# Encoder layer on one core: half of the input projection as twelve unit pairs by seven block products, values with 512 moving columns, chains moved beside keys, queries and gates

## The chip, the cores and the metric

The kernel runs on one core of a Trainium2 chip. The metric is the device time of one execution in microseconds; the median of several runs counts. The engines are called as in the profile: PE or TensorE for matmuls (PEld for its weight loads), DVE or VectorE, ACT or ScalarE, POOL or GpSimd, SP or SyncE. The last two, and ScalarE at times, issue DMAs.

## The reference

One encoder layer is applied to two request groups that share the weights: a prompt of 256 tokens and a sample of 1024 tokens, with 1024 channels, in float32.

```python
h = rmsnorm(x, g_mix_pre)
z = h @ w_in                                  # 1024 x 9216
rq, rk, rv, rg, pin, mq, gl = jnp.split(z, list(IN_SPLITS), axis=-1)
gates = jax.nn.sigmoid(gl)                    # three gates of 1024 channels
y_ret = retention_branch(rq, rk, rv, rg, decay_fwd, decay_bwd, ret_gn) @ w_ret_out
y_pool = pool_branch(pin, pool_w, pool_scale) @ w_pool_out
y_mem = memory_branch(mq, mem, g_mem, w_mem_kv) @ w_mem_out
merged = gates[:, :, 0] * y_ret + gates[:, :, 1] * y_pool + gates[:, :, 2] * y_mem
x = x + rmsnorm(merged @ w_o, g_mix_post)
x = x + rmsnorm(conv_ffn(rmsnorm(x, g_ffn_pre), w_up, conv_w, conv_b, w_down), g_ffn_post)
```

Retention has 4 heads of 256 channels, rotary positions on q and k, and a decay in both directions; its output is normalised per head and multiplied by silu(rg). Pooling takes means over windows of 2, 4, 8 and 16 tokens minus the token, in four groups of 256 channels, each followed by a 256 x 256 product. The memory branch is softmax attention of mq over 256 memory tokens, whose keys and values come from `w_mem_kv`.

## The kernel before

**Numbers and matmuls.** Every float32 operand x is split into hi = x rounded to the short float format (`hilo`: a ScalarE copy) and lo = x - hi (a VectorE subtraction). `mm3` makes one product of three matmuls, hi x hi, hi x lo and lo x hi, on lines 148 to 150. All 1280 tokens are handled together (`T`), as the groups 512, 512 and 256 of `GROUPS`.

**Weights.** `Weights` streams the weight units (128 x 1024) in a fixed order, the list `srcs`: loaded by SP into two raw tiles, split into a ring of four (lines 87 and 88). A unit is taken when it is needed (`take`), and `tick` refills the ring, so that in steady work one unit is split at the first tick of each unit.

**Feature-major units.** One unit gives 128 output columns for all tokens: three groups of 24 matmuls with the weight as the stationary side (`fm_groups`), 48 with 512 and 24 with 256 moving columns. Values are token-major: per head and per pair of token tiles, 48 matmuls with 256 moving columns (memory values likewise, line 470).

**Chains in the background.** While TensorE works through units, generators in `bg` take one step at each `tick`, and so put their matmuls between the groups. All is issued in this order; nothing is reordered later. `drain` ticks until `bg` is empty. The stages, in order:

1. Memory keys (8 units) and memory values; beside them the statistics of x and the split inputs `hT`, and the decay tables (`decay_tables`), `dtab` among them.
2. `mq` units (8) and values (4 x 2 units); beside them `mem_chain`: 20 jobs of scores, softmax, transposes and the product with the values.
3. `pool_unit` x 8, `rotary_unit` x 4 for q, x 4 for k; beside them `pool_chain`. Its step for one half of a group makes log2(w) shifted sums, edge products, a difference and a split; the products with `pool_w` follow when both halves are there.
4. `rg` units (8); beside them `state_chain`, 16 jobs.
5. 24 gate units; beside the first 22 `ret_chain`, 20 chunks (4 heads x 5). After three preparing steps each chunk takes two, `scores` and (`transp` of the chunk before) `output` with `split` of the next chunk behind it. The tick after the third group is left out for the chain (line 960), but in the first unit.
6. The three branches' output projections, `w_o`, then the MLP. Its up-projection multiplies the sample's 2 x 2 blocks (two halves of tokens, two of channels, a gate unit and a value unit) with seven products instead of eight, on weight sums that stand in DRAM.

**Weight sums.** `sums` makes `s12_d` and `s34_d` for the 22 pairs of up-projection units in five stages per pair, one stage per tick: two DRAM to DRAM copies by SP, then four accumulating DMAs by POOL, each two rounds behind the one that it needs.

**Banks.** `ps_mm` has four PSUM banks for units, `ps_ch` four for chains.

Of the kernel before, what the change touches and what calls it, by code (L numbers as in the profile page):

```python
# [8 lines left out]
F32 = mybir.dt.float32  # L9
# [8 lines left out]
P = 128  # L18
# [20 lines left out]
PCOLS = PW - 2 * PAD  # L39
SLOT = 2 * T  # L40
# [18 lines left out]
class Weights:  # L59
# [8 lines left out]
    def load(self):  # L68
        if self.n_load < self.load_limit and self.n_load < self.n_split + self.RAW:
            t = self.pool.tile([P, 1024], F32, tag="wr", name="wr", bufs=self.RAW)  # L70
            self.nc.sync.dma_start(out=t, in_=self.srcs[self.n_load])
            self.raw[self.n_load] = t
            self.n_load += 1
# [22 lines left out]
    def take(self, n=1):  # L96
# [7 lines left out]
        return out  # L104

# [5 lines left out]
def encoder(ctx: ExitStack, tc: tile.TileContext, a: dict):  # L111
# [68 lines left out]
    w_in = a["w_in"]  # L180
    srcs = [a["w_kv"][i] for i in range(16)]
    srcs += [w_in[40 + i] for i in range(8)]
    srcs += [w_in[16 + i] for i in range(8)]
    for h in range(H):
        srcs += [w_in[32 + 2 * h], w_in[33 + 2 * h], w_in[2 * h], w_in[2 * h + 1]]
    srcs += [w_in[8 + i] for i in range(8)]
    srcs += [w_in[24 + i] for i in range(8)]
    srcs += [w_in[48 + i] for i in range(24)]
# [4 lines left out]
    s12_d = [dram.tile([P, 2, 512], F32, name=f"s12d{q}") for q in range(NF)]  # L193
    s34_d = [dram.tile([P, 2, 512], F32, name=f"s34d{q}") for q in range(NF)]
# [4 lines left out]
    for nm, q in stream:  # L199
        srcs.append({"u0": a["w_up"][q], "a2": a["w_up"][NF + q],  # L200
                     "s12": s12_d[q][:].rearrange("p a b -> p (a b)"),
                     "s34": s34_d[q][:].rearrange("p a b -> p (a b)")}[nm])
# [24 lines left out]
    vm_d = [dram.tile([P, 4, HD], F32, name=f"vm{h}") for h in range(H)]  # L227
    q_d = [dram.tile([P, NCH, 2, C], F32, name=f"qd{h}") for h in range(H)]
    k_d = [dram.tile([P, NCH, 2, C], F32, name=f"kd{h}") for h in range(H)]
    v_d = [dram.tile([P, NCH, 2, HD], F32, name=f"vd{h}") for h in range(H)]  # L230
# [12 lines left out]
    def sums():  # L243
        lag = 2

        def stage(i, q):
            u, v = (a["w_up"][n].rearrange("p (a b) -> p a b", b=512) for n in (q, NF + q))
            both = lambda x: x.unsqueeze(1).to_broadcast([P, 2, 512])
            s12, s34 = s12_d[q], s34_d[q]
            if i == 0:  # L250
                nc.sync.dma_start(out=s12[:], in_=both(v[:, 0, :]))
                nc.sync.dma_start(out=s34[:], in_=u)
            elif i == 1:
                nc.gpsimd.dma_start(out=s12[:], in_=both(v[:, 1, :]), accum_op=ALU.add)
            elif i == 2:
                nc.gpsimd.dma_start(out=s34[:, 0, :], in_=v[:, 0, :], accum_op=ALU.add)
            elif i == 3:
                nc.gpsimd.dma_start(out=s12[:, 1, :], in_=u[:, 0, :], accum_op=ALU.add)
            else:
                nc.gpsimd.dma_start(out=s34[:, 1, :], in_=s12[:, 1, :], accum_op=ALU.add)  # L260

        for n in range(NF + 4 * lag):
            for i in range(5):
                q = n - lag * i
                if 0 <= q < NF:
                    stage(i, q)
                    yield

    summing = [None]

    def tick(step=True):
        ws.tick()
        if summing[0] is not None:
            next(summing[0], None)
# [13 lines left out]
    ds = ExitStack()  # L288
    dec = ds.enter_context(tc.tile_pool(name="dec", bufs=1))
# [62 lines left out]
    def x_stats():  # L352
# [15 lines left out]
        xrb = s0.tile([P, T], F32, name="xrb")  # L368
# [27 lines left out]
    dtab = dec.tile([P, H, 2, C], F32, name="dtab")  # L396

    def decay_tables():
# [24 lines left out]
        nc.vector.tensor_scalar(out=kd, in0=kd, scalar1=HD ** -0.5, scalar2=None, op0=ALU.mult)  # L423
        yield
        rel = s0.tile([P, 2, 2 * C], F32, name="rel")
        nc.sync.dma_start(out=rel, in_=a["rel"])
        for h in range(H):
# [6 lines left out]
            yield  # L434

# [4 lines left out]
    with tc.tile_pool(name="st0", bufs=3) as stp:  # L440
# [21 lines left out]
        for h in range(H):  # L462
            w2 = ws.take(2)
            for j in range(2):
                b = mmb(2, HD)
                for i in range(2):
                    ts = slice((2 * j + i) * P, (2 * j + i + 1) * P)
                    for c in range(KC):
                        wh, wl = (w[:, (c % 4) * HD:(c % 4 + 1) * HD] for w in w2[c // 4])
                        mm3(b[:, i, :], memT[c][:, 0, ts], memT[c][:, 1, ts], wh, wl, c == 0, c == KC - 1)  # L470
                o = stp.tile([P, TM], F32, tag="st", name="st")
                for i in range(2):
                    nc.scalar.activation(o[:, i * HD:(i + 1) * HD], b[:, i, :], AF.Copy,
                                         scale=mrs[:, 2 * j + i:2 * j + i + 1])
                nc.gpsimd.dma_start(out=vm_d[h][:, 2 * j:2 * j + 2, :],
                                    in_=o[:].rearrange("p (a b) -> p a b", b=HD))
                tick()
# [18 lines left out]

# [1262 lines left out]
```

## Time and profile before

| what | value |
|---|---|
| median of 3 runs | 2686.07 us (2685.98 to 2686.65) |
| the profiled execution's own time | 2684.68 us |
| its span, first to last instruction | 2682.9 us |
| mean granted TensorE clock | 0.996 |
| busy: PE, PEld | 2644.3 us (99%), 2293.8 us (85%) |
| busy: DVE, ACT, POOL | 1351.0 us (50%), 919.0 us (34%), 279.2 us (10%) |
| DMA | 397.58 MB, mean 148 GB/s |

Busy time of PE counts overlapping matmuls once. A matmul's own length (0.39 us for 512 columns) is longer than the distance to the next one, since matmuls overlap; the cost of one is that distance. The granted clock is given as a share of 2.4 GHz.

### The profile page before, as it was taken

Reading aid. Unit: us, or ns where it says so; the run is one execution under the profiler, and the core shown is the slowest. Engines: PE = TensorE matmul, PEld = TensorE weight load, DVE = VectorE, ACT = ScalarE, POOL = GpSimd, SP = SyncE. Lnnn points to the kernel's source line nnn. Section 1 sums busy time; section 2 is a strip of 40 time slices with the busy share of each in tenths; the row PEclk is TensorE's granted clock in tenths of the full one; section 3 lists DMA queues with packets and bytes.
Section 4 is the critical chain, followed back from the end, with each engine's and each line's share of the span. In section 5 each row is a group of like instructions: output and inputs, shape, how many; then the busy total and the mean of one; then the engine's idle time right before and its main releaser. Section 6 shows DMA issues by size and latency. Waiting matters only on the chain.

```text
span 2682.9 us, 36263 instructions
## 1 busy us (share of the span) xinstructions
PE 2644.3 (99%) x14396; PEld 2293.8 (85%) x14396; DVE 1351.0 (50%) x2267; ACT 919.0 (34%) x1567; POOL 279.2 (10%) x457
## 2 busy tenths in 40 slices
PE   8999999999999999999999999999999999999998
PEld 6999998888888888888888888777888888878786
DVE  5645303445445355555423453567666566554454
ACT  5433311221124333232312021665344444434333
POOL 1111221211123111111100000110000000000000
PEclk9999999999999999999999999999999999999999
DMA  7775566665478544444434353453333333353443
GB/s 262 260 193 143 138 158 159 153 166 138 126 177 218 167 147 163 138 155 154 155 105 149 111 156 102 145 177 99 113 111 111 113 116 106 128 184 127 149 147 110
DMA packets 145435, 397.58 MB, mean 148 GB/s; under 512 B 17680, under 2 KB 27792, under 8 KB 144912
## 3 DMA queue, kind: packets, MB, share of 16 engines
q1 hardware_dynamic: 100128, 267.02, 30.9%
q0 software_dynamic: 44848, 127.95, 17.6%
q8 instruction: 113, 1.85, 0.3%
q14 instruction: 58, 0.48, 0.1%
q10 hardware_dynamic: 288, 0.28, 0.0%
HBM read 303.69 MB, written 143.39 MB: 167 GB/s over the span
## 4 chain that ended last, share of the span: by engine, by line
PE 93%; DMA 2%; DVE 2%; ACT 2%; issue 1%; SPq 0%; POOL 0%; DVEq 0%; ACTq 0%; POOLq 0%
PE f L1316 15%; PE mm L149 13%; PE mm L148 13%; PE mm L150 13%; PE f L150 10%; PE f L149 10%; PE f L148 10%; PE ch L149 3%; PE ch L150 3%; PE ch L148 3%; DMA wr<-w_kv_in 1%; DMA x<-x2d 0%; DVE wl L88 0%; PE ch L559 0%; PE f L1142 0%
## 5 line engine op out<-in xcount | busy, mean ns | idle before, releaser
L148 PE MATMUL mm<-b,wh 128*128 128x512 f32 (+1 forms) x1536 | 545.7, 355 | 0.0
L149 PE MATMUL mm<-b,wh 128*128 128x512 f32 (+1 forms) x1536 | 544.3, 354 | 0.0
L150 PE MATMUL mm<-b,wl 128*128 128x512 f32 (+1 forms) x1536 | 543.6, 354 | 0.0
L88 DVE TENSOR_TENSOR wl<-wr,wh 128x1024 fp32r<-128x1024 f32 x244 | 297.7, 1223 | 411.6 <-ACT wh L87 407.3
L87 ACT ACTIVATE wh<-wr 128x1024 fp32r<-128x1024 f32 x244 | 255.2, 1050 | 281.5 <-PE f L149 150.7
L150 PEld LDWEIGHTS mm<-b,wl 128*128 128x128 f32 x1536 | 290.1, 189 | 40.9
L148 PEld LDWEIGHTS mm<-b,wh 128*128 128x128 f32 x1536 | 290.4, 189 | 39.1
L149 PEld LDWEIGHTS mm<-b,wh 128*128 128x128 f32 x1536 | 290.4, 189 | 38.3
L1316 PE MATMUL f<-b,wh 128*128 128x512 f32 x880 | 273.9, 393 | 0.0
L1316 PEld LDWEIGHTS f<-b,wh 128*128 128x128 f32 x880 | 161.9, 189 | 30.7
L1316 PE MATMUL f<-b,wl 128*128 128x512 f32 x440 | 171.7, 390 | 0.0
L150 PE MATMUL f<-wh,gl 128*128 128x512 f32 x390 | 153.3, 393 | 5.7 <-DVE gl L141 5.5
L148 PE MATMUL f<-wh,gl 128*128 128x512 f32 x390 | 152.8, 392 | 1.5 <-ACT gl L140 1.5
L149 PE MATMUL f<-b,wh 128*128 128x512 f32 (+1 forms) x432 | 153.4, 355 | 0.0
L148 PE MATMUL f<-b,wh 128*128 128x512 f32 (+1 forms) x432 | 153.1, 354 | 0.0
L150 PE MATMUL f<-b,wl 128*128 128x512 f32 (+1 forms) x432 | 152.8, 354 | 0.0
L149 PE MATMUL f<-wl,gl 128*128 128x512 f32 x390 | 152.7, 392 | 0.0
L141 DVE TENSOR_TENSOR gl<-b,gl 128x640 fp32r<-128x640 f32 x78 | 63.9, 825 | 116.2 <-ACT gl L140 116.1
L964 ACT ACTIVATE gate<-mm 128x512 f32<-128x512 f32 (+1 forms) x68 | 35.5, 522 | 223.6 <-PE mm L150 132.9
L140 ACT ACTIVATE gl<-b 128x640 fp32r<-128x640 f32 x78 | 57.3, 739 | 158.6 <-PE f L150 152.0
L1316 PE MATMUL f<-hc,wh 128*128 128x512 f32 x352 | 108.9, 391 | 0.0
L148 PE MATMUL f<-h2p,wh 128*128 128x256 f32 x352 | 99.9, 284 | 3.3 <-ACT h2p L140 3.3
(343 smaller groups left out, 5295.4 us busy)
## 6 DMA issues: line engine op xcount, KB each, us to landing
wr<-w_in_in SPq DMA_DIRECT2D x72, 512.0 KB, 3.9
wr<-w_up_in SPq DMA_DIRECT2D x44, 512.0 KB, 3.6
wr<-w_down_in SPq DMA_DIRECT2D x44, 512.0 KB, 3.6
b<-fgd SPq DMA_DIRECT2D x44, 320.0 KB, 4.8
h2s<-gtd SPq DMA_DIRECT2D x48, 256.0 KB, 3.8
s12d<-w_up_in SPq DMA_DIRECT2D x22, 512.0 KB, 6.4
s34d<-w_up_in SPq DMA_DIRECT2D x22, 512.0 KB, 7.4
s12d<-w_up_in POOLq DMA_DIRECT2D x22, 512.0 KB, 7.5
```

The lines of the kernel that those rows point to most:

```text
L87: self.nc.scalar.activation(h, r[:], AF.Copy)
L88: self.nc.vector.tensor_tensor(out=l, in0=r[:], in1=h.bitcast(F32), op=ALU.subtract)
L140: nc.scalar.activation(hi, src, AF.Copy)
L141: nc.vector.tensor_tensor(out=lo, in0=src, in1=hi.bitcast(F32), op=ALU.subtract)
L148: nc.tensor.matmul(out, ah, bh, start=first, stop=False)
L149: nc.tensor.matmul(out, ah, bl, start=False, stop=False)
L150: nc.tensor.matmul(out, al, bh, start=False, stop=last)
L964: nc.scalar.activation(y[:, 0:n], b, AF.Sigmoid)
L1316: nc.tensor.matmul(b, w[x][:, ks], hterm(nm, c, y), start=first and c == k == 0, stop=last and c == 3 and k == 2, skip_group_check=True)
```

## The change

Three things are changed. (1) The units of `mq`, `pin` and `rg` (24 of 72) become twelve pairs ("quads"), worked before all chains: on the sample tokens by seven block products of 12 matmuls with 512 columns, on the prompt plainly. Their weights are the first unit, the last unit and two sums made in DRAM by the same `sums` as before, which now has 34 pairs; a load of a sum runs the generator until that sum is complete. Results go through DRAM (`mq_d`, `pin_d`, `g_d`), the block terms of the tokens are made from `xT` while the values are computed (`in_terms`). (2) Values and memory values are computed with 512 moving columns, four, one, one and four token tiles at a time (`token_major`). (3) The chains move: memory beside keys (k) and one gate, pooling and the decay matrix beside nine gates, states beside q, retention beside the gates that are left. Keys and queries tick after each group of each unit; beside the retention chain a gate unit also steps in the middle of its first group (`mid`) and after every group.

```diff
+    def hold(self, i):
+        while self.n_split <= i:
+            assert self.can_split()
+            self.split()
+        return self.hl[i]
+
+    def free(self, i):
+        self.hl.pop(i)
+        self.n_taken += 1
+        self.n_done += 1
+        self.split()
...
+    def sum_of(d, q):
+        def src():
+            while q not in summed:
+                next(summing)
+            return d[q][:].rearrange("p a b -> p (a b)")
+        return src
...
+    N_MEM, N_POOL = 1, 9
...
+    def token_major(base, lhs, nt, out):
+        blocks = [range(4)] if nt == 4 else [range(4), (4,), (5,), range(6, nt)]
+        for p in range(2):
+            ids = [base + 4 * p + i for i in range(4)]
+            for g, ts in enumerate(blocks):
+                bs = {t: (mmb if len(ts) > 1 else chb)(512) for t in ts}
+                for i, u in enumerate(ids):
+                    wh, wl = ws.hold(u)
+                    for t in ts:
+                        for c in range(2):
+                            k, cs, cols = 2 * i + c, slice(t * P, (t + 1) * P), slice(c * 512, (c + 1) * 512)
+                            mm3(bs[t], lhs[k][:, 0, cs], lhs[k][:, 1, cs], wh[:, cols], wl[:, cols],
+                                k == 0, k == KC - 1)
+                        if i == 3:
+                            out(p, t, bs[t])
+                    if g == len(blocks) - 1:
+                        ws.free(u)
+                    if len(ts) > 1 or i == 3:
+                        tick()
...
-    def fm_groups(wh, wl, src, groups=GROUPS):
+    def fm_groups(wh, wl, src, groups=GROUPS, mid=None):
         for o, n in groups:
             b = mmb(n)
             for c in range(KC):
+                if mid and o == 0 and c == KC // 2:
+                    mid()
...
+        def release(nm, q):
+            ws.free(quad_at + 4 * q + ("u0", "s12", "s34", "a2").index(nm))
+            sum_step(2)
...
+        for q in range(NQ):
+            d, more = Q[q], q + 1 < NQ
+            product(d["a"], unit("s12", q, 1), "T2", False, True)
+            u2 = snap(qtile("u2", 2)[:], d["a"])
+            pr(q, 0, 1)
+            d["d"] = mmb(512)
+            product(d["d"], unit("s34", q, 0), "T3", True, True)
+            product(d["a"], unit("s12", q, 0), "T1", False, True)
+            u4 = snap(qtile("u4", 1)[:], d["a"])
+            release("s12", q)
+            pr(q, 1, 1)
+            close(q, 1, TP + HS, minus, d["d"], u4)
+            if more:
+                p1(q + 1)
+            product(d["a"], unit("s34", q, 1), "B22", False, True)
+            emit(q, 0, TP + HS, HS, d["a"])
+            release("s34", q)
+            if more:
+                pr(q + 1, 0, 0)
+            product(d["d"], unit("a2", q, 1), "T4", False, True)
+            close(q, 1, TP, minus, d["d"], u2)
+            release("a2", q)
+            if more:
+                pr(q + 1, 1, 0)
+                p2(q + 1)
...
+            o, n, b1 = next(g1)
+            tick()
+            _, _, b2 = next(g2)
...
     bg.append(mem_chain())
+    cs_ = rotary_consts(mp)
     for h in range(H):
+        rotary_unit(k_d[h], mp, *cs_)
+    for _ in range(N_MEM):
+        gate_unit(mp)
...
     bg.append(pool_chain())
+    bg.append(decay_matrix(pp))
+    for _ in range(N_POOL):
+        gate_unit(pp)
...
+    with tc.tile_pool(name="rtp", bufs=1) as rp:
+        bg.append(ret_chain(rp))
+        while bg and gate_n[0] < 23:
+            gate_unit(rp, stepped)
+        drain()
```

In the pooling chain a yield now follows each of the two halves of a group's products, where there were two before for each; in the states' and the memory chain the starting yields become fewer. `split_q` of the memory chain has one buffer instead of two and reads from DRAM. An output of a pair goes through one of five tiles (`qo`); for `rg` a sigmoid takes a second of the five.

## Rows read from the trace of the kernel before

**Rows 1.** The page: busy time of the engines, and one costly group.
```profile
PE 2644.3 (99%) x14396; PEld 2293.8 (85%) x14396; DVE 1351.0 (50%) x2267; ACT 919.0 (34%) x1567; POOL 279.2 (10%) x457
...
L87 ACT ACTIVATE wh<-wr 128x1024 fp32r<-128x1024 f32 x244 | 255.2, 1050 | 281.5 <-PE f L149 150.7
```
**Rows 2.** TensorE's waits, first and last of 16: us, times, longest.
```profile
PE f L150 <- DVE gl L141: 5.5, 2, 3.3
...
PE ch L150 <- DVE wl L88: 0.2, 1, 0.2
```
**Rows 3.** TensorE's timeline, two groups of 24 matmuls and what follows: start, us, instruction.
```profile
189.45 0.40 PE L148 MATMUL mm<-b,wh 128*128 128x512 f32 x1
...
194.92 0.28 PE L148 MATMUL ch<-pt,vhl 128*128 128x256 f32 x1
...
198.22 0.28 PE L148 MATMUL mm<-b,wh 128*128 128x256 f32 x1
...
201.10 0.28 PE L148 MATMUL ch<-pt,vhl 128*128 128x256 f32 x1
```
**Rows 4.** The chain that ended last, two pairs of the up-projection.
```profile
1845.97 5.47 PE f L1316 x24
...
1870.85 5.47 PE f L1316 x24
```
**Rows 5.** TensorE's timeline, one retention chunk.
```profile
1063.08 0.28 PE L148 MATMUL ch<-qkvhl 128*128 128x256 f32 x1
...
1069.98 0.60 PE L931 MATMUL ch<-ident,y 128*128 128x128 f32 x4
...
1074.59 0.28 PE L148 MATMUL mm<-b,wh 128*128 128x256 f32 x1
...
1082.93 0.28 PE L148 MATMUL ch<-qkvhl 128*128 128x256 f32 x1
```
**Rows 6.** VectorE's timeline, the same chunk.
```profile
1074.79 1.00 DVE L912 SCALAR_TENSOR_TENSOR y<-ch,qdec,y 128x256 f32<-128x256 f32 x2 [0.28 <-PE ch L150]
...
1079.94 1.88 DVE L141 TENSOR_TENSOR qkvhl<-qkvr,qkvhl 128x512 fp32r<-128x512 f32 x3
1084.76 1.23 DVE L88 TENSOR_TENSOR wl<-wr,wh 128x1024 fp32r<-128x1024 f32 x1 [2.93 <-ACT wh L87]
1085.90 0.68 DVE L882 TENSOR_TENSOR str<-ch,dtab 128x512 f32<-128x512 f32 x1
1087.34 0.69 DVE L141 TENSOR_TENSOR sthl<-str,sthl 128x512 fp32r<-128x512 f32 x1 [0.76 <-ACT sthl L140]
```
**Rows 7.** VectorE's timeline, one half of a pooling group (window 2).
```profile
427.21 1.52 DVE L664 TENSOR_TENSOR ps<-pin 128x1310 f32<-128x1310 f32 x1
...
431.89 1.51 DVE L141 TENSOR_TENSOR dh<-ps,dh 128x1296 fp32r<-128x1296 f32 x1 [1.35 <-ACT dh L140]
```
**Rows 8.** VectorE's timeline, one memory step.
```profile
188.95 0.69 DVE L141 TENSOR_TENSOR pt<-ch,pt 128x512 fp32r<-128x512 f32 x1 [0.78 <-ACT pt L140]
...
192.45 0.68 DVE L141 TENSOR_TENSOR qhl<-mq,qhl 128x512 fp32r<-128x512 f32 x1
```
**Rows 9.** TensorE's timeline, its longest wait; in brackets the wait.
```profile
2373.41 0.79 PE L150 MATMUL f<-wh,gl 128*128 128x512 f32 x1 [3.27 <-DVE gl L141]
```
**Rows 10.** Windows: busy (x) per engine, then PEclk, DMA share, GB/s.
```profile
340.00:400.00 60.00, 60.00 (x502) 60.00 (x502) 4.72 (x4) 10.37 (x15) 13.06 (x18) 1.00 0.67 165
960.00:1320.00 360.00, 360.00 (x2097) 318.35 (x2097) 200.84 (x541) 108.92 (x188) 45.01 (x77) 1.00 0.44 143
770.00:840.00 70.00, 70.00 (x387) 60.71 (x386) 32.24 (x58) 30.21 (x63) 22.53 (x33) 1.00 0.85 219
...
2373.00:2379.00 6.00, 5.59 (x13) 4.44 (x14) 2.96 (x4) 0.00 (x0) 0.44 (x1) 0.50 0.82 246
```
**Rows 11.** POOL's timeline, the second stage of two successive sums.
```profile
337.33 1.14 POOL L254 DMA_DIRECT2D s12d<-w_up_in  x1
...
366.13 1.13 POOL L254 DMA_DIRECT2D s12d<-w_up_in  x1
```

More of the change, by code (lines that the diff above doesn't have):

```diff
@@ L39 @@
 PCOLS = PW - 2 * PAD
+PWA = 1408
 SLOT = 2 * T
@@ L183, in encoder @@
     srcs += [w_in[16 + i] for i in range(8)]
[L184 to L188, printed above, removed]
+    quad_at = len(srcs)
+    for q in range(NQ):
+        srcs += [quad_srcs(nm, q, 0) for nm in ("u0", "s12", "s34", "a2")]
+    gates = [w_in[48 + i] for i in range(24)]
+    srcs += [w_in[8 + i] for i in range(8)] + gates[:N_MEM + N_POOL]
@@ L189, in encoder @@
+    srcs += [w_in[i] for i in range(8)] + gates[N_MEM + N_POOL:]
     srcs += [a["w_mem_out"][i] for i in range(8)]
@@ L241, in encoder, with sum_step @@
     bg = []
[L243 to L269, printed above, removed]
+    def sum_step(n=1):
+        for _ in range(n):
+            next(summing, None)
+    adding = [False]
     def tick(step=True):
         ws.tick()
-        if summing[0] is not None:
-            next(summing[0], None)
+        if adding[0]:
+            sum_step()
         for g in list(bg) if step else ():
@@ L461, in encoder, with mem_v @@
             tick()
[L462 to L477, printed above, removed]
+        def mem_v(p, j, b):
+            o = stp.tile([P, TM], F32, tag="st", name="st")
+            nc.scalar.activation(o, b, AF.Copy, scale=mrs[:, j:j + 1])
+            nc.gpsimd.dma_start(out=vm_d[p][:, j], in_=o[:].rearrange("p (a b) -> p a b", b=HD))
+        ws.n_done = ws.n_taken
+        token_major(8, memT, 4, mem_v)
     drain()
     p0.close()
-    def fm_groups(wh, wl, src, groups=GROUPS):
+    def fm_groups(wh, wl, src, groups=GROUPS, mid=None):
         for o, n in groups:
@@ L576, in mem_chain @@
         load_k(0)
+        load_q(0)
+        load_q(1)
         load_v(0)
-        for _ in range(4):
-            yield
+        yield
+        yield
         split_k(0)
-        split_v(0)
-        while 0 not in mq:
-            yield
         split_q(0)
         yield
+        split_v(0)
         n = len(jobs)
@@ new lines, in encoder, with gate_out, gate_unit @@
+    gate_n = [0]
+    def gate_out(m, pool, o, n, b):
+        y = pool.tile([P, 512], F32, tag="gate", name="gate", bufs=3) if pool else stile(n)
+        nc.scalar.activation(y[:, 0:n], b, AF.Sigmoid)
+        nc.gpsimd.dma_start(out=gate_d[m][:, o:o + n], in_=y[:, 0:n])
+    def gate_unit(pool, mid=None):
+        m = gate_n[0]
+        gate_n[0] += 1
+        (wh, wl), = ws.take()
+        for o, n, b in fm_groups(wh, wl, hT, mid=mid):
+            gate_out(m, pool, o, n, b)
+            tick()
@@ L610, in encoder, with stepped @@
+    def stepped():
+        for g in list(bg):
+            try:
+                next(g)
+            except StopIteration:
+                bg.remove(g)
     bg.append(mem_chain())
-    summing[0] = sums()
+    cs_ = rotary_consts(mp)
     for h in range(H):
-        while h >= 2 and h - 2 not in mq_done:
-            tick()
-        t = mp.tile([P, 2, T], F32, tag="mq", name="mq", bufs=2)
-        for e in range(2):
-            (wh, wl), = ws.take()
-            for o, n, b in fm_groups(wh, wl, hT):
-                nc.vector.tensor_copy(t[:, e, o:o + n], b)
-                if e == 1 and o == GROUPS[-1][0]:
-                    mq[h] = t
-                tick()
@@ L812, in state_chain @@
         load(1)
-        for _ in range(4):
-            yield
+        yield
+        yield
         for n in range(len(jobs) + 1):
```

380 lines of the change are left out of this document (235 added, 145 removed).

## The prediction

> **What bounds the kernel now.** I read the page first, for one engine that is full; then TensorE's waits, for what that engine waits for; then its timeline, for what a matmul really costs; and last VectorE's timeline in the stages to which work is moved. The page puts TensorE at 99% of the span and VectorE at 50% [rows 1]. The 16 entries of TensorE's waits come to 30 us together, the longest 5.5 us and the shortest 0.2 us [rows 2]. So TensorE's instruction stream sets the time, stage by stage: a matmul less is time saved, and any wait put into that stream is time lost, one for one.
>
> Matmuls overlap, so the length of one is not its cost; the distance between starts is. 24 matmuls with 512 moving columns take 194.92 - 189.45 = 5.47 us, 0.228 each; 24 with 256 take 201.10 - 198.22 = 2.88 us, 0.120 each [rows 3]. A unit (128 output columns, all tokens) is thus 5.47 + 5.47 + 2.88 = 13.8 us of cover for the chains beside it.
>
> **What the change saves.** *Seven products.* Twelve pairs of units took 96 matmuls of 512 columns each on the sample tokens; seven block products of 12 matmuls are 84. 144 matmuls x 0.228 = 32.8 us. The up-projection already runs this scheme with four half-products on the prompt: 24.88 us from one pair to the next [rows 4], where two plain units take 27.6, and 12 x 2.76 = 33 us agrees. *Values.* 10 x 4 x 8 x 3 = 960 matmuls of 256 columns become 480 of 512, and in the memory values 384 become 192. 672 x (2 x 0.120 - 0.228) = 7.9 us. The Trainium skill, "TensorE: Matmul & The Clock Gate", section "Wait — 56ns, not 53.3ns?", has columns / 2.4 GHz plus some 2.5 ns from start to start, which would make this second saving an estimated 1.8 us; the rows have larger steps, and I keep the rows. Total: 41 us less of TensorE, 40 to 44.
>
> **What is put into the stream.** *Retention chain.* Before, 22 gate units covered its 20 chunks, two steps per unit. Ten gates now go to the memory and pooling chains, so 13 are left, and the chain takes four steps per unit: in the middle of the first group and after each group. A chunk has two steps, scores and output, and behind its output VectorE works in this order: state multiply-adds, statistics, the small operations of rsqrt, normalisation, then the splits of k, q and v for the next chunk. The next scores need the k and q splits.
> In the rows, scores of one chunk start at 1063.08, its output step at 1069.98, the next TensorE work at 1074.59, the next scores at 1082.93 [rows 5]. VectorE starts its last multiply-adds at 1074.79 and the three splits at 1079.94, taking 1.88 us for three [rows 6]: q is ready at about 1081.2, 6.6 us after the output step. Before, 8.34 us of gate matmuls lay in between, 1.7 us too much; that is why the chain cost nothing. Three steps pass before the first scores, so the first scores fall on the fourth step of a unit, and every output step after that falls on the middle or on the second group's end. What follows the output is then half a group (12 x 0.228 = 2.73 us) or the short group (2.88 us). Chunks with fewer states have two or four multiply-adds less, so I take 6.3 us as their mean. Each of 19 transitions waits 6.3 - 2.8 + some 0.1 for the semaphore = 3.6 us: 68 us. The other half, scores to output, holds: the decay product starts at 1085.90 and the split that output needs ends at 1087.34 + 0.69 [rows 6], 2.1 us, against 2.73 or more. The weight split (1.23 us, [rows 6]) stands behind the q split and delays no scores. Queued behind a waiting scores matmul is everything on TensorE. Bounds: 55 us if the mean is 5.7 us, 80 us with 7.
>
> *Pooling chain.* Its 24 steps shared 48 ticks with eight units and eight rotary pairs; now 27 ticks of nine gates, and the decay table (four steps) is made there too. The product of a window needs both halves' differences. One half with one shift is a serial stretch from 427.21 to 433.40, VectorE, ScalarE, VectorE: 6.2 us [rows 7]. Each further shift is another 1.52 us and two edge products some 0.3. Where a half's first step shares a tick with a weight split, the split leads by some 2.5 us (ScalarE 1.05, [rows 1], VectorE 1.23, [rows 6]). Between a first half and the product lie two intervals, 5.47 + 2.88 = 8.3 us. Window 2: 12.4 plus the table's operations (some 2.6 us between the halves) against 8.3: 7 us. Window 4: 2.5 + 2 x 8.0 = 18.5: 10 us. Windows 8 and 16, which have three and four intervals: 2.5 + 14.6 against 13.8, and 26 against 19.3: 3 and 7 us. Sum 27; bounds 15 and 45, the upper if the first load comes late.
>
> *Memory and state chains.* Beside rotary pairs each second tick has six VectorE operations on 512 columns, about as long as the decay product of that size (0.68 us, [rows 6]), ahead of the chain. A memory step runs from its first split to its last in 192.45 + 0.68 - 188.95 = 4.2 us [rows 8]; with 4.1 of rotary ahead, 8.3 us. TensorE's own step (two products of 12 x 0.120 and the transposes, 3.2), the next group (5.47) and the product before the transposes (1.4) cover 10.1 us, or 7.5 where the group is short. Some five short ones and the head changes wait a microsecond or so. The same sum for states gives about 3 us. Together 8; bounds 2 and 20.
>
> *Clock.* After its longest wait, 3.27 us [rows 9], the granted clock was 0.50 from 2373 to 2379, that is 1.2 GHz, and 13 matmuls of 512 columns took 5.59 us [rows 10], 0.43 each instead of 0.228: 2.6 us lost. The retention waits are as long, but shorter matmuls follow them; at 1.2 to 1.5 us a time, 16 or so of them and four pooling waits are 26 us. Below: 8, if most do not reach the lower level. Above: 40.
>
> *DMA.* Block sums of the weights are made in DRAM. One sum (five stages) passes in 366.13 - 337.33 = 28.8 us beside value work [rows 11]. From 340 to 400 the sixteen engines are busy 0.67 x 60 = 40.2 us [rows 10]. Two units of 0.52 MB and five stores of 0.26 MB per sum are 4.9 MB there, at the rate of 960 to 1320 (0.44 at 143 GB/s, no sums, [rows 10]: 3.1 us per MB) 15 us. The other 25 us, over 2.08 sums, are 12 us each. A pair of units now advances the sums by 8 stages, 1.6 sums, 19.3 us; its four weight tiles and its outputs are 3.4 MB, 10.5 us. That is 29.8 us of DMA in 24.9 us of TensorE. What is late first is the store of an output behind the sums on POOL's queue; behind it the output buffer (five), ScalarE, the bank, TensorE. Nothing (at a share of 0.85, 770 to 840, TensorE waits for nothing, [rows 10]) to 12 x 4.9 = 59 us. The buffers absorb some 20 and the kept rows show no harm at 0.85, so I take 20. The pumped start (16 stages at once, ahead of the first sum's load on SP) lies beside values with half their 109 us left, and costs nothing while that cover lasts; gone, it would be up to 10 us.
> The extra 24 weight splits (1.23 us, [rows 6], and 1.05 us, [rows 1]), the terms made from xT, the copies and the sigmoids lie on engines under 60% beside values and pairs; the up-projection has the same load and no waits. Unhidden, the terms would cost some 30 us.
>
> **Sum**, against the profiled execution's own 2684.7 (its span is 2682.9 and 1.8 lie around it; the median of the runs is 1.4 above it): 2684.7 - 41 + 68 + 27 + 8 + 26 + 20 = 2792.7; with the 1.4, about **2794 us**, 4.0% slower.
>
> **Rivals.**
> *The chain stays hidden (faster).* One mechanism decides it: whether the q split lands within 2.8 us of the output step. If it does, the retention wait and its clock loss vanish, and with pooling mostly covered by VectorE running ahead the time is 2686 - 41 = 2645, a few microseconds more with small waits. For it: VectorE is at 50%, and TensorE waits nowhere today. Against it: 6.6 us is a dependent stretch in one engine's order, not a load. Chance 0.09.
> *Waits come, but the clock and the DMA do not follow.* 2686 - 41 + 68 + 15 + 5 = 2733, down to 2710 with the lower bounds. For it: the share of 0.85 in [rows 10]. Chance 0.16, and in it and the next one about 0.03 of no measurable change.
> *Transfers bind the pairs.* All 59 us are paid, and pooling's upper bound: 2686 - 41 + 68 + 45 + 8 + 30 + 59 = 2855. The Trainium skill, "DMA: Bandwidth & Descriptors", section "Issuing engines are not separate DMA queues", has SP's and POOL's transfers share the same sixteen engines; by that rule the 29.8 us count in full. The shares in [rows 10] add up as the rule says, yet none there is above 0.85. Chance 0.12.
> *As forecast*, between 2740 and 2840: 0.63.
>
> **Numbers.** A difference of 0.2% (5.4 us) is about what a measurement of this kernel can tell from none. Faster 0.09, same 0.03, slower 0.88. The range reaches into the second and third rivals, from 2705 to 2855, and leaves out the fast one and the far end of the last.
>
> **What would show it.** Waits of TensorE for VectorE's split qkvhl, some 19 of about 3.6 us, and for dh, four; a granted clock under 1 in those stages; 12 pairs in 12 x 24.9 us if the DMA does not bind, and a share near 1 there if it does. Matmul counts lower by 144 + 672. I am wrong if qkvhl is not among the waits, or if a wait that I left out (a sum's load on SP, the terms at the first pair) is.

## The result, and the profile after

The changed kernel takes 2838.2 us (2837.0 to 2842.3, four runs) against 2686.0 us for the kernel before in the same series: a ratio of 1.057, 95% interval 1.0555 to 1.0586. That is 152 us slower. The forecast was 2794, in a range of 2705 to 2855.

The page of the changed kernel first: span, then busy times.

```profile
span 2836.0 us, 35229 instructions
PE 2660.5 (94%) x13580; PEld 2267.7 (80%) x13580; DVE 1420.0 (50%) x2343; ACT 982.5 (35%) x1637; POOL 351.7 (12%) x553
```

Beside [rows 1]: 816 matmuls fewer, which is 144 + 672 as counted from the diff, and yet TensorE is busy for 16 us longer and idle for 2836.0 - 2660.5 = 175.5 us, where it was 38.6. Busy time does not tell work here, since matmuls at the lower clock start further apart (0.42 us instead of 0.23, below). Counted in the trace, 118.3 us of the busy time lie in stretches with a granted clock of 0.50 (1.2 GHz), against 18.9 before. Half of that is lost: 59.1 and 9.5 us. (The half is borne out by e10_four below, which has the matmuls of the kernel before: 74.2 us more at 0.50, 38.7 us more of busy time.) What remains, the work at full clock, is 2601.3 against 2634.8 us. So the 153.1 us between the two spans are +136.9 of waiting, +49.6 of clock and -33.5 of work.

TensorE's waits name the places (us in total, times, longest):

```profile
PE ch L163 <- DVE qkvhl L155: 62.4, 19, 3.7
PE ch L162 <- ACT dh L154: 29.8, 6, 6.1
PE mm L162 <- ACT vst L614: 18.0, 3, 9.0
PE ch L162 <- ACT qhl L154: 7.7, 1, 7.7
PE mm L162 <- ACT st L523: 7.7, 3, 5.1
PE f L164 <- DVE gl L155: 7.1, 2, 3.8
PE ch L163 <- DVE dh L155: 6.0, 6, 1.2
...
PE mm L637 <- ACT q L567: 2.8, 2, 1.7
```

Of these only the wait of the MLP for `gl` stood in [rows 2]. The first is retention, `dh` is pooling, `vst` and `st` are the stored values and memory values, `qhl` is the head of the memory chain, `q` the outputs of the pairs.

Windows of four stages (values, pairs, pooling, retention) show where the clock fell; columns as in [rows 10]. The DMA share adds up the times of packets, so it can pass 1.

```profile
118.00:253.00 135.00, 117.03 (x495) 95.65 (x495) 40.84 (x49) 29.47 (x45) 33.62 (x45) 0.91 0.93 251
253.00:548.00 295.00, 291.55 (x1542) 251.00 (x1540) 92.95 (x103) 88.31 (x129) 108.00 (x143) 1.00 1.04 279
775.00:960.00 185.00, 149.26 (x718) 125.01 (x718) 76.26 (x89) 60.18 (x82) 36.00 (x76) 0.89 0.42 122
1125.00:1455.00 330.00, 267.65 (x1438) 234.27 (x1437) 195.66 (x541) 89.50 (x156) 29.20 (x48) 0.90 0.40 130
```

The pairs have the fullest DMA engines of all, a share of 1.04, and the full clock. The three stages with a clock near 0.9 are those with TensorE idle for 18, 36 and 62 us.

One retention chunk on TensorE, as in [rows 5]; in brackets the wait:

```profile
1152.70 0.39 PE L163 MATMUL ch<-qkvhl 128*128 128x256 f32 x1 [3.01 <-DVE qkvhl L155]
...
1154.12 0.41 PE L162 MATMUL ch<-qkvhl 128*128 128x256 f32 x1
1154.33 0.41 PE L163 MATMUL ch<-qkvhl 128*128 128x256 f32 x1
...
1154.76 0.63 PE L162 MATMUL mm<-b,wh 128*128 128x512 f32 x1
1155.18 0.63 PE L163 MATMUL mm<-b,wh 128*128 128x512 f32 x1
...
1157.04 0.40 PE L162 MATMUL mm<-b,wh 128*128 128x512 f32 x1
1157.27 0.40 PE L163 MATMUL mm<-b,wh 128*128 128x512 f32 x1
```

And VectorE ahead of it, as in [rows 6]:

```profile
1150.71 0.74 DVE L1141 TENSOR_SCALAR y<-y,ag,rsy 128x256 f32<-128x256 f32 x2
1151.36 1.89 DVE L155 TENSOR_TENSOR qkvhl<-qkvr,qkvhl 128x512 fp32r<-128x512 f32 x3
```

The splits follow the normalisation without a gap, and the scores follow q's split. Behind the wait the starts of matmuls are 0.21 us apart instead of 0.12 (256 columns) and 0.42 instead of 0.23 (512 columns), until some 4 us after the wait. The wait costs 3 us itself and about 1.7 us of clock behind it.

### The profile page after: what moved, and what is told of

It reads as the page before. It is cut to its first block, busy times and chain, and to the rows that moved or that the text cites. A ratio compares the mean times of both kernels' runs of the same rounds, so it can differ in the third digit from the quotient of the medians.

```text
span 2836.0 us, 35229 instructions
## 1 busy us (share of the span) xinstructions
PE 2660.5 (94%) x13580; PEld 2267.7 (80%) x13580; DVE 1420.0 (50%) x2343; ACT 982.5 (35%) x1637; POOL 351.7 (12%) x553
## 4 chain that ended last, share of the span: by engine, by line
PE 66%; DVE 9%; DMA 5%; issue 3%; ACT 3%; POOL 0%; SPq 0%; DVEq 0%; ACTq 0%; POOLq 0%
PE f L1510 14%; PE f L164 10%; PE f L162 10%; PE f L163 10%; PE mm L162 5%; PE mm L163 5%; PE mm L164 5%; PE ch L163 3%; PE ch L164 2%; PE ch L162 2%; DMA gd<-q 1%; DMA wr<-w_in_in 1%; DVE qkvhl L155 1%; DVE wl L90 1%; ACT wh L89 1%
## 5 line engine op out<-in xcount | busy, mean ns | idle before, releaser
L90 DVE TENSOR_TENSOR wl<-wr,wh 128x1024 fp32r<-128x1024 f32 x268 | 327.5, 1224 | 525.1 <-ACT wh L89 520.3
L89 ACT ACTIVATE wh<-wr 128x1024 fp32r<-128x1024 f32 x268 | 280.6, 1050 | 304.0 <-PE f L163 155.5
L162 PE MATMUL mm<-b,wh 128*128 128x512 f32 (+1 forms) x960 | 350.8, 365 | 0.0
L163 PE MATMUL mm<-b,wh 128*128 128x512 f32 (+1 forms) x960 | 347.6, 362 | 0.0
L164 PE MATMUL mm<-b,wl 128*128 128x512 f32 (+1 forms) x960 | 345.7, 360 | 0.0
L164 PEld LDWEIGHTS mm<-b,wl 128*128 128x128 f32 x960 | 186.4, 194 | 27.7
L162 PEld LDWEIGHTS mm<-b,wh 128*128 128x128 f32 x960 | 187.6, 195 | 25.6
L163 PEld LDWEIGHTS mm<-b,wh 128*128 128x128 f32 x960 | 187.3, 195 | 25.0
L162 PE MATMUL f<-b,wh 128*128 128x512 f32 (+1 forms) x432 | 153.1, 355 | 0.0
L637 PE MATMUL mm<-tt,wh 128*128 128x512 f32 x384 | 119.1, 391 | 2.8 <-ACT q L567 2.8
```

The lines of the kernel that those rows point to most:

```text
L89: self.nc.scalar.activation(h, r[:], AF.Copy)
L90: self.nc.vector.tensor_tensor(out=l, in0=r[:], in1=h.bitcast(F32), op=ALU.subtract)
L162: nc.tensor.matmul(out, ah, bh, start=first, stop=False)
L163: nc.tensor.matmul(out, ah, bl, start=False, stop=False)
L164: nc.tensor.matmul(out, al, bh, start=False, stop=last)
L637: nc.tensor.matmul(b, w[x][:, ks], in_term(nm, c, y), start=first and c == k == 0, stop=last and c == 3 and k == 2, skip_group_check=True)
```

## The experiments

Time saved is told against the changed kernel's profiled span of 2836.0 or its median of 2838; a ratio is to the kernel before. "Clock" is half of the matmul time at 0.50, counted as above.

**The splits ahead of the statistics (e1_split).**

```diff
+            split(n + 1)
+            load(n + 2)
             if n:
                 transp(n - 1)
             output(n)
-            split(n + 1)
-            load(n + 2)
```

> One edit: in the retention chain the splits of the next chunk's k, q and v (and the loads behind them) are emitted at the head of the output step, ahead of the gate transposes, the state multiply-adds and the statistics of the present chunk. Theory (dependent stretch: q's split stands on VectorE behind the statistics): the 19 waits for qkvhl, 62 us, go to under 5 us, the stage 1115 to 1455 shrinks by those and by its lost clock (granted 0.90 there, some 25 us of TensorE's busy time), so 2838 - 62 - 25 = about 2751 us; up to 20 us may come back as waits for the decayed scores, whose product now stands behind the statistics instead: 2751 to 2771. Rival 1 (VectorE as a whole is too slow for four steps per unit): the waits only change their tile, their sum stays at 50 us or more, time above 2815. Rival 2 (the loads of q from DRAM are late): qkvhl stays, above 2815. Rival 3 (waits go, the clock does not come back): 2776.

Measured: 2743.7 us, ratio 1.0206 (1.0189 to 1.0223). `qkvhl` is gone from TensorE's waits; the decayed scores, which now come behind the statistics, wait this little:

```profile
PE ch L164 <- DVE sthl L155: 0.4, 2, 0.2
...
PE ch L162 <- ACT sthl L154: 0.4, 2, 0.2
```

The window of the stage has a clock of 1.00 and TensorE busy for 264.2 of 265 us, at a higher VectorE load than before the edit (75% instead of 59%):

```profile
1115.00:1380.00 265.00, 264.20 (x1607) 235.62 (x1606) 198.41 (x564) 94.59 (x168) 32.83 (x55) 1.00 0.53 178
```

The span is 100.9 us shorter: 69.6 less idle and 29.5 less lost to the clock, the rest work. So the loss was the order of VectorE's queue, not its load, nor the loads from DRAM.

**The same steps one place later (e2_shift).**

```diff
         split(0)
         load(1)
         yield
+        yield
```

> One edit: one more preparing step in the retention chain, so that output steps fall on the ends of the first and the third group instead of the middle of the first and the end of the second. What follows an output step is then a group of 5.46 us or a half group of 2.73 us, in turn, instead of 2.73 or 2.88. Theory (a wait is 6.2 us less what lies behind the output step): ten waits fall to 0.7 us, nine stay at some 3.4: 38 us instead of 62 for qkvhl, and half of the stage's lost clock comes back (12 us): about 2802 us. Rival (the waits are set by loads or by VectorE's whole load, not by the place of the step): 62 us stay, 2838.

Measured, in a single execution: 2794.4 us. `qkvhl` waits 40.7 us in all; the waits alternate between some 0.9 and some 3.4 us, as long matmul groups and short ones follow the output step in turn; 11.4 us of clock come back. The wait is a fixed stretch less what TensorE has to do meanwhile.

**TensorE kept at work in the wait (e3_fill).**

```diff
+            if n:
+                f = chb(2, C)
+                for i in range(24):
+                    nc.tensor.matmul(f[:, 0, :], hT[i % KC][:, 0, 0:P], hT[0][:, 0, 0:C], start=True, stop=True)
             b = chb(2, C)
```

> Added work: 24 matmuls of 256 columns into a chain bank of their own, whose result nothing reads, ahead of the scores of chunks 1 to 19, so that TensorE multiplies while the split of q is on its way. At 0.120 us each they are 2.9 us, as long as the mean wait of 3.28. Theory (idle TensorE is what lowers the granted clock): waits for qkvhl fall to some 10 us, the clock of the stage rises from 0.90 to 0.98 or more, TensorE executes 456 matmuls more and the kernel is still faster, 2805 to 2818 us. Rival (the clock is lowered by something else, or comes back by itself): clock stays at 0.90, the added matmuls cost more than they fill, 2838 to 2890.

Measured: 2808.0 us, ratio 1.045 (1.042 to 1.048). TensorE has 53.4 us more work at full clock and the kernel is 30 us faster: idle falls by 56.9 us, filled by that work, and 26.6 us of clock come back. The stage:

```profile
1125.00:1466.00 341.00, 333.39 (x2112) 299.98 (x2111) 210.72 (x573) 103.94 (x179) 33.59 (x56) 1.00 0.44 149
```

This separates the two prices of a wait: the idle time was paid in useless matmuls, and what was gained is the clock.

**One part of the change alone, in the kernel before (e10_four).**

```diff
...
-        for o, n, b in fm_groups(wh, wl, hT):
+        for o, n, b in fm_groups(wh, wl, hT, mid=stepped if step else None):
             gate_out(m, pool, o, n, b)
-            tick(step and (n == 512 or m == 0))
+            tick(step)
```

> The kernel before with one part of the change alone: its retention chain takes four steps per gate unit (in the middle of the first group and behind each group) instead of two, over eleven units; the other gates follow without a chain. Nothing else is changed. Theory (the loss of the retention stage comes from the place of the steps, not from the block products, the sums or the 512 columns): 19 waits for qkvhl of 3.3 us, 62 us, and some 25 to 33 us of clock: 2686 + 62 + 29 = about 2777 us. Rival (the waits need the new kernel's transfers or loads): 2686, no change.

Measured: 2784.4 us, ratio 1.036 (1.0344 to 1.0376). Without pairs, without 512-column values and without more sums:

```profile
PE ch L149 <- DVE qkvhl L141: 62.3, 19, 3.7
```

The same 19 waits, to 0.1 us. 97 us of the 152 are the four steps per gate unit and nothing else of the change.

**Pooling, one more step (e4_pool).**

```diff
-    N_MEM, N_POOL = 1, 9
+    N_MEM, N_POOL = 1, 10
...
                 load(2 * g + c + 2)
                 yield
+            yield
             for e in range(2):
...
-    bg.append(decay_matrix(pp))
...
         bg.append(state_chain(rp))
+        bg.append(decay_matrix(rp))
```

> Pooling alone: one more step between a window's second half and its products (28 steps instead of 24), ten gates beside it instead of nine, and the decay table's four steps moved to the state stage. Theory (a serial stretch of VectorE and ScalarE behind each half, with too little TensorE work between): waits for dh from 36 us to 8 or less, the granted clock in that stage from 0.89 to 0.97 or more, some 20 us: 2838 - 28 - 20 = about 2790 us. Rival 1 (the halves' loads from DRAM are late, so that a later step only waits less by what it is later): 15 us or more stay, 2815. Rival 2 (moving the table to the state stage makes waits there): the gain there is taken back, above 2825.

Measured: 2826.5 us, ratio 1.0519 (1.0503 to 1.0535): a quarter of the gain that was expected. `dh` still waits 16.5 us. ScalarE shows why in the first window: the pooling weights are late, and VectorE's sums stand behind their split.

```profile
773.74 0.63 ACT L154 ACTIVATE pwh<-pwr 128x512 fp32r<-128x512 f32 x1 [7.79 <-DMA pwr<-pool_w_in]
```

And a new wait has come at the end of retention:

```profile
PE f L162 <- ACT gate L867: 13.1, 1, 13.1
```

The tenth gate in pooling was one of the two plain gate units behind the retention chain. They cover the load of the memory branch; with one of them gone, ScalarE splits that branch ahead of the last gates, and TensorE waits 13.1 us for their banks.

**Pooling, products one half later (e7_pipe).** The order of the steps, as rewritten, with the weights loaded one window ahead and the table moved as above:

```python
for g in range(H):
    yield from half(g, 0)
    if g:
        products(g - 1, 0)
        yield
        products(g - 1, 1)
        yield
    split_w(g + 1)
    yield from half(g, 1)
```

> Pooling alone, a second way: the products of a window are emitted behind the first half of the next window (three buffers for the halves' differences instead of two), the 256 x 256 pooling weights are loaded one window ahead, and the decay table is made in the state stage; the gates stay nine, the steps 25. Theory (serial stretch of VectorE and ScalarE ahead of the products; what stayed in the kernel with one more step were late pooling weights, 8.3 us from issue to the split): waits for dh from 36 to 5 us or less, the granted clock of the stage from 0.89 to 0.98, some 20 us, and no new wait at the end of the retention stage since all its gates are there: 2838 - 31 - 20 = about 2787. Rival (the halves' own loads are late): 15 us stay, 2815.

Measured: 2798.4 us, ratio 1.0413 (1.0396 to 1.0431). `dh` waits 2.5 us, idle is 36.4 us less, the span 35.8: the theory of the stretch holds. The 20 us of clock do not come. In pooling only 19.7 us of matmuls had run at 0.50 (9.9 us lost), and 6.8 still do; the clock of a window is a mean over its idle time too, and I had read it as lost work. Over the whole kernel the clock costs 3.5 us more than before this edit.

**The sums begun earlier (e5_sums).**

```diff
...
+        adding[0] = 2
         ws.n_done = ws.n_taken
         token_major(8, memT, 4, mem_v)
...
```

> One edit: the block sums of the weights begin in the memory values (two stages at each of its eight ticks), ahead of the sample values, where they go on at one stage a tick; so the first sum is done when its load is issued on SP, and SP is not held. Theory 1 (SP, held from 173 to 197 by the load of the first sum, brought the last x tile of the terms late, and with it VectorE, ScalarE and the value evictions): the third wait for vst (9.0 us) goes, the first two (5.6 and 3.4) stay, as do their stores; with half of the lost clock of the stage (12 us in all): 2838 - 9 - 6 = about 2823 us. Theory 2 (saturated DMA engines: the stores of the values are late wherever the sums start): 18 us stay, 2838. Bad case: the sums now delay the stores of the memory values, 2845.

Measured: 2840.6 us, ratio 1.0568 (1.0552 to 1.0583), no change. `vst` falls from 18.0 to 6.0 us, so SP's wait for the first sum did delay the values. But `st` rises from 7.7:

```profile
PE mm L162 <- ACT st L523: 25.4, 4, 15.0
```

POOL's timeline shows what came ahead: two stages of a sum wait for their predecessors, and x loads and then the stores of the memory values stand behind them.

```profile
81.86 1.09 POOL L214 DMA_DIRECT2D s12d<-w_in_in  x1 [16.49 <-DMA s12d<-w_in_in]
83.95 0.55 POOL L372 DMA_DIRECT2D xr<-xT_in  x1 [1.00 <-DVE b L158]
85.53 1.09 POOL L214 DMA_DIRECT2D s12d<-w_in_in  x1 [1.03 <-DMA s12d<-w_in_in]
87.94 0.55 POOL L372 DMA_DIRECT2D xr<-xT_in  x1 [1.32 <-DVE b L158]
88.48 1.63 POOL L524 DMA_DIRECT2D vm<-st  x3
```

The wait was moved, not removed.

**The input projection's sums left out (e6_nosum).**

```diff
-        for n in range(len(sum_rows) + 4 * lag):
+        for n in range(NQ, len(sum_rows) + 4 * lag):
...
+        if not at:
+            nm = {"s12": "u0", "s34": "a2"}.get(nm, nm)
...
```

> The input projection's twelve block sums are not made: in place of a sum, a plain weight row of the same size is loaded (so mq, pin and rg are other numbers; the amount of work on every compute engine is the same), and the sums of the up-projection are made from the key stage on, one stage a tick. It prices the DMA work of those sums. The forecast's own term: 20 us, 2818; its upper bound, in which the transfers bind the pairs: 59 us, 2779. From the trace of the changed kernel: the waits that can come from it are vst 18, q 2.8 and the first chunk of the memory chain 7.7, with some 12 us of clock in the value stage: 40 us at most, 2798; if only part of these come from the transfers, 2815.

Measured: 2811.0 us, ratio 1.046 (1.0444 to 1.0476), 27 us less than with them. The pairs, with and without sums (295 us each):

```profile
235.00:530.00 295.00, 295.00 (x1559) 254.70 (x1558) 96.31 (x107) 91.73 (x133) 38.38 (x71) 1.00 0.40 137
```

A share of 0.40 instead of 1.04, and the twelve pairs take 290.0 us from their first product to their last instead of 294.3. But e7_pipe, whose pairs and sums are those of the changed kernel, needs 290.1 us for them, and TensorE is all but fully busy:

```profile
253.00:548.00 295.00, 294.54 (x1566) 254.47 (x1565) 94.09 (x104) 91.08 (x134) 109.02 (x145) 1.00 1.02 281
```

So full DMA engines cost the pairs between nothing and 4.3 us. The rest went at their two ends: `vst` falls to 2.8 us, `qhl` and `q` vanish. `st` stays, at 8.6 us.

**All fixes together (e8_all, e9_best, e11_last).** The edits of e1_split and e7_pipe, a step more at the head of the memory chain, and three ways to spread the sums. The first is that of e5_sums:

```diff
...
     bg.append(mem_chain())
+    next(bg[0])
     cs_ = rotary_consts(mp)
...
         load_v(0)
         yield
         yield
+        yield
...
```

> Together: q, k and v splits at the head of the output step, pooling products one half later with early weights, the decay table in the state stage, the sums begun in the memory values, and one more preparing step at the head of the memory chain, whose loads go ahead of the rotary tables on SP. Theory (the change itself saves 41 us of TensorE, all the rest was waits and the clock that follows them): 2838 - 95 (retention, as measured) - 51 (pooling) - 15 (values) - 8 (memory chain) = about 2669 us, 0.6% faster than before. Rival 1 (only the retention and pooling fixes work): 2692, no faster than before. Rival 2 (removing these uncovers other waits, the DMA engines' in the pairs above all): above 2710.

Measured: 2710.8 us, ratio 1.009 (1.0075 to 1.0105), 42 us above the theory. Retention and pooling wait for next to nothing, but the sums hold up the start as in e5_sums, and the memory chain its first keys:

```profile
PE mm L162 <- ACT st L523: 24.5, 4, 15.1
PE ch L163 <- DVE khl L155: 8.9, 1, 8.9
```

The second holds the load of the first sum back, gives the stores of the values and memory values more buffers, and makes the terms of the tokens in other steps:

```diff
...
-            t = pool.tile([P, TS], F32, tag="xs", name="xs", bufs=3)
+            t = pool.tile([P, TS], F32, tag="xs", name="xs", bufs=2)
...
-            o = vp.tile([P, 512], F32, tag="vst", name="vst", bufs=2)
+            o = vp.tile([P, 512], F32, tag="vst", name="vst", bufs=4)
...
-        adding[0] = True
+        adding[0] = 13
+        ws.load_limit = quad_at + 1
...
```

> The combined kernel once more, with another start of the sums: in the values two stages a tick for thirteen ticks and then none until the pairs, the load of the first sum held back for as long, six stages a pair instead of eight and the rest of the up-projection's sums beside keys, pooling, queries and gates; four buffers each for the stored memory values and values, two instead of three for the x tiles of the terms. Theory (what is left of the combined kernel's loss is stores and loads that land late while the engines of the DMA are full: 24.5 us in the memory values, 6.1 in the values, 11.8 at the head of the memory chain, and the clock after them): these fall to some 15 us together, the granted clock to 0.99: 2711 - 27 - 8 = about 2676 us, 0.4% faster than before. Rival (the transfers are only moved again): 2700 or more.

Measured: 2699.5 us, ratio 1.0045 (1.0033 to 1.0058), 23 us above the theory. Memory values and values wait only 8.7 us together, and now pooling waits for `dh` and its output buffers, 19.4 us, beside the sums that were put there, and the memory chain 7.2 us for `khl`. The last version puts them beside the pairs (seven stages each), the keys and the retention chain, and has one more step at the head of the memory chain:

```diff
...
-            sum_step(2 if nm in ("s12", "a2") else 1)
+            sum_step(1 if nm == "u0" else 2)
...
-    adding[0] = 1000
+    adding[0], pace[0] = 27, 1
...
+        adding[0] = 1000
         bg.append(ret_chain(rp))
```

> The last combined kernel with the up-projection's sums spread another way: seven stages a pair instead of six, one a tick beside the keys, none beside pooling and queries, the rest beside the retention chain; and one more preparing step at the head of the memory chain. Theory (its waits in pooling, 12 us for dh and 7 for the output buffer, and one of 3.3 in the states come from the sums' transfers that now run beside them, since the same chains wait some 3 us where no sums run; 7.2 us at the head of the memory chain from a split that comes one step too soon): these 30 us fall to some 10, the clock gives 6 back: 2699 - 20 - 6 = about 2673 us, 0.5% faster than before. Rival (they are latencies of the chains, or the retention stage now waits for its loads instead): 2695 to 2710.

Measured: 2671.5 us, ratio 0.9943 (0.9929 to 0.9957): 0.6% faster than the kernel before.

```profile
span 2666.5 us, 35233 instructions
PE 2614.1 (98%) x13580; PEld 2237.2 (84%) x13580; DVE 1414.9 (53%) x2343; ACT 971.5 (36%) x1631; POOL 352.7 (13%) x553
```

Against before: work at full clock -39.7 us, clock +9.5, idle +13.8. The change's saving was there all the time; the waits and the clock behind them stood on top of it.

## Why the prediction was right, point by point

The mechanism was right: a dependent stretch in VectorE's order, uncovered because the steps come closer together, and a clock that follows the waits. The sum came out 44 us short of the measured time:

| term | forecast | measured in the changed kernel |
|---|---|---|
| products and values | -41 | -33.5 of work at full clock |
| retention waits | +68 | +62.4, 19 of 3.28 |
| pooling | +27 | +35.8 for `dh` |
| memory and state chains | +8 | +5.3 (`pr` 3.2, `khl` 1.1, `v1hl` 1.0) |
| DMA | +20 | +28.5 (`vst` 18.0, `qhl` 7.7, `q` 2.8) |
| clock | +26 | +49.6 |
| all other waits | 0 | +5.0 (`st` 7.7, the rest -2.7) |
| sum | +108 | +153 |

`qhl` stands under DMA and `st` does not, since without the sums (e6_nosum) `qhl` is gone and `st` is not. The clock alone is 24 of the 44 us.

*The step that was mis-sized is the clock:* "at 1.2 to 1.5 us a time, 16 or so of them and four pooling waits are 26 us". Its upper bound of 40 was too low as well. The 19 retention waits led to 17 stretches at 0.50 with 64.0 us of matmuls in them, the scores and the head of the next half group: 32 us lost, 1.7 for each wait. Pooling lost 9.9 us in the same way, the values 7.1, the rest of the kernel 10.1, which is about what the whole kernel lost before (9.5). e3_fill shows the cause: fill the waits and 26.6 us come back. I had weakened the term by "shorter matmuls follow them"; what counts is time at the lower clock, and shorter matmuls are then only more in number.

*Retention.* The 3.6 us were 3.28; places and number as worked out. e1_split, e2_shift and e10_four show it from three sides. The rival "the chain stays hidden" needed a q split within 2.8 us of the output step. That is what e1_split makes: the retention wait and its clock loss vanish as that rival said, and only the other losses stay.

*Pooling.* 35.8 is inside the bounds of 15 to 45, but not spread as worked out. For the windows of 2, 4, 8 and 16 tokens TensorE waits 13.7, 13.2, 2.6 and 6.2 us, where I had 7, 10, 3 and 7. The excess lies in the two short windows. Ahead of the first, ScalarE stood for the pooling weights,

```profile
775.85 0.63 ACT L154 ACTIVATE pwh<-pwr 128x512 fp32r<-128x512 f32 x1 [7.45 <-DMA pwr<-pool_w_in]
```

and from 781.78 to 817 us, between the halves of the first and ahead of the second, the decay table was made, with eight loads of ScalarE's function table (last section). The upper bound was for a late first load; e7_pipe removes late weights, table and dependent stretch at once and does not tell their shares.

*DMA.* The size was near (27 us by e6_nosum), but that was luck, since the place was wrong. I had the outputs of the pairs pay it; they lost 4.3 us here and nothing in e7_pipe. "The pumped start ... costs nothing while that cover lasts" failed: SP held that load for 23.8 us,

```profile
SPq L73 <- DMA s12d<-w_in_in: 23.8, 1, 23.8
```

the last x tile behind it was issued at 198.51 us, ScalarE stood 28.29 us for VectorE's scaling of it, and the evictions of the values came behind:

```profile
216.34 0.63 ACT L154 ACTIVATE tt<-xs 128x512 fp32r<-128x512 f32 x1 [28.29 <-DVE xs L556]
...
222.84 1.07 ACT L614 ACTIVATE vst<-mm 128x512 f32<-128x512 f32 x2
```

That is the 9.0 us wait, near the 10 us that I had named for cover gone, and in part the sign of being wrong that I had named, a sum's load on SP. The TensorE work beside it was no cover, since it needed banks that ScalarE had not emptied. The first of the other two `vst` waits (5.6 us) has the same form, without a sum: an x tile issued at 159.80 us was there for VectorE at 168.36, and ScalarE's evictions stood behind it. The second (3.4 us) is two buffers for stores, one of which ScalarE awaited for 7.00 us:

```profile
170.28 0.63 ACT L154 ACTIVATE tt<-xs 128x512 fp32r<-128x512 f32 x1 [6.74 <-DVE xs L556]
...
180.88 0.60 ACT L614 ACTIVATE vst<-mm 128x512 f32<-128x512 f32 x1 [7.00 <-DMA vd<-vst]
```

`st`, a wait that I had left out, is not the sums' doing: four tiles of memory values are emptied at once into three buffers, and their stores were issued on POOL at 85.78 us, behind a load of x that had waited for VectorE. The Trainium skill, "DMA: Bandwidth & Descriptors", section "Issuing engines are not separate DMA queues", has transfers of all issuers share the same engines; the share of 1.04 in the pairs agrees. The rival built on it, that transfers bind the pairs, fell all the same: a share of 1.04 over 24.5 us is 25.5 us of transfers a pair, where I had 29.8. I had named 12 pairs in 12 x 24.9 us as the sign of no binding and a share near 1 as the sign of it, and both came. That buffers absorb some 20 us, as I had assumed, no run shows.

*The saving.* By work at full clock it is 33.5 us in the changed kernel and 39.7 in the last version. The seven products pay as forecast: pairs start 24.88 us apart, as in [rows 4],

```profile
280.83 0.39 PE L637 MATMUL mm<-tt,wh 128*128 128x512 f32 x1
...
305.71 0.39 PE L637 MATMUL mm<-tt,wh 128*128 128x512 f32 x1
```

where nothing waits. The values pay too: 24 matmuls took 2.88 us with 256 columns (values, the kernel before), and 24 take 5.44 us with 512 (memory values, the changed kernel),

```profile
340.08 0.28 PE L149 MATMUL mm<-wl,b 128*128 128x256 f32 x1
...
342.96 0.28 PE L149 MATMUL mm<-wl,b 128*128 128x256 f32 x1
```

```profile
62.47 0.39 PE L162 MATMUL mm<-wh,memT 128*128 128x512 f32 x1
...
67.91 0.39 PE L162 MATMUL mm<-wh,memT 128*128 128x512 f32 x1
```

which is 0.120 and 0.227 us each, and 672 x (2 x 0.120 - 0.227) = 8.7 us. The Trainium skill's rule for the distance of matmuls ("TensorE: Matmul & The Clock Gate", section "Wait — 56ns, not 53.3ns?") made this second saving an estimated 1.8 us; the traces do not agree with it. What makes 33.5 too small is the count of busy time: the last matmul ahead of every stop counts with its whole length as the profile models it, 0.39 us where the distance is 0.23. TensorE's matmuls form 72 stretches without a gap in the changed kernel, 26 in the kernel before and 43 in the last version. With the distance in place of the length at their ends, the work falls by 43.2 us in the changed kernel and by 42.5 in the last one, inside the forecast's 40 to 44. The 9.7 us between 33.5 and 43.2 belong to the stops: the waits cost that much more than the table says.

What stays open: what late weights, table and dependent stretch each cost in pooling, what held the clock at full behind two of the 19 retention waits, and how much of e11_last's remaining 13.8 us of idle time could still be removed.

## What to carry to other kernels

When background work is packed more tightly, compare each step's dependent stretch, in the order of the engine that runs it, with the foreground work that is left between two steps. The engine's load says nothing about it: the retention stage waited at a VectorE load of 59% and no longer at 75%, and moving three operations to the head of a step was worth 95 us here. Count a wait of TensorE with the slow matmuls behind it, half as much again in this kernel. Before starting a DMA chain that waits on itself, list what stands behind it on its queue, and price it at the stages before and after the one that it serves.

## What the runs showed that I had not expected

- Behind 17 of the 19 retention waits, each of 2.9 to 3.7 us, the granted clock fell to 0.50, and it came back while TensorE was still in the half group behind the scores; the stage as a whole was not slowed, only the head of what followed each wait.
- DMA engines at a share of 1.02 to 1.04 for 295 us cost TensorE between nothing and 4.3 us, while an accumulating DMA that waited for its predecessor held POOL's queue for 16.5 us.
- Making the decay table beside sigmoids switches ScalarE's function table to and fro between the exponential and the sigmoid: nine loads of 1.28 us on these two lines in the changed kernel, 11.5 us of ScalarE.

```profile
L867 ACT ACT_TABLE_LOAD x5 | 6.4, 1283 | 0.1
L471 ACT ACT_TABLE_LOAD x4 | 5.1, 1283 | 0.1
```

The Trainium skill, "ScalarE activation tables: per-element evaluation and per-set limits", section "What a function is on this engine", has functions of different sets one such load of 1283 ns apart; the trace agrees. I had priced the table at some 2.6 us between the halves, without them.
